# A hybrid decoder block on one core: scores of two heads in turn on two halves of TensorE's rows, PSUM pools of 3, 4 and 1 banks, a weight load moved up

## The chip, the core and the metric

The kernel runs on one core of one Trainium2 chip. The metric is the device time of one execution in microseconds; shown times are medians of a few runs. Engines are named as the profile names them: PE (matmul; PEld is its weight load), DVE, ACT, POOL, and SP, which here only issues DMAs. PSUM has eight banks, into which PE writes; a bank holds 512 fp32 numbers in each of its 128 partitions.

## What is computed

One decoder block over 16 meta tokens and 512 tokens of width 2048, all in fp32. One input projection feeds a state-space mixer (S5) and attention of 16 heads of 64; both results are normalised, concatenated, projected back, and a gated MLP with a short causal convolution follows. The part that the change touches most is attention, which is stick-breaking instead of softmax:

```python
def _stick_breaking_block(q_blk, qpos, k, v, kpos):
    scale = 1.0 / math.sqrt(ATTN_HEAD_DIM)
    z = jnp.einsum('bqhd,bkhd->bhqk', q_blk, k).astype(jnp.float32) * scale
    valid = (kpos[None, :] < qpos[:, None])[None, None]
    log_keep = jnp.where(valid, jax.nn.log_sigmoid(-z), 0.0)
    suffix = lax.cumsum(log_keep, axis=3, reverse=True) - log_keep
    w = jnp.where(valid, jnp.exp(jax.nn.log_sigmoid(z) + suffix), 0.0)
    return jnp.einsum('bhqk,bkhd->bqhd', w.astype(v.dtype), v)
...
        proj = hn @ w_in[i]
        u = proj[..., :SSM_WIDTH]
        q, k, v = jnp.split(proj[..., SSM_WIDTH:], 3, axis=-1)
...
        mixed = jnp.concatenate([rmsnorm(y_ssm, g_ssm_out[i]), rmsnorm(y_attn, g_attn_out[i])], axis=-1)
        h = h + mixed @ w_out[i]
```

## The kernel before

All activations lie with channels on the partitions and the 528 positions along the free dimension. An fp32 product is made of three matmuls on a rounded part and a remainder of each factor: high by high, high by low, low by high (`mm3`, L320 to L322). Weights come as blocks of 128 x 1024; ACT rounds a block (L242, `wh<-wr`), DVE takes the remainder (L117, `wl<-wr,wh`). `dense` runs over the blocks of one output tile of 128 channels, its positions as two halves of 256 to 264, so that a block is used for 48 matmuls.

The order of everything is written out by hand; no scheduler moves an instruction, and each engine works its own queue in order. What isn't dense work (the S5 mixer, then attention) is a generator, a *lane*. After nearly each trio of dense matmuls `pulse` adds 1.4 ns per column to a credit, and for each `period` of credit it takes one step of the lane. `PERATT` is that period in attention. While `hold` is set, during the last Q projection and the GLU of the mixer, the lane stands still.

Attention goes by four units of four heads (two pairs p, in a pair the heads i = 0, 1, whose 64 channels lie on partitions 0 to 63 and 64 to 127). `prep` splits K and Q into high and low parts and transposes V. A unit's items are: chunk 0 of the queries with all heads, chunk 1 with heads 0 and 1, then 2 and 3, chunks 2 and 3 with each head alone, and None for the last 16 queries. With chunk j go 128(j+1) keys. An item passes through
- `stage_a`: PE puts a mask into a bank of the pool psz (L961) and adds the scores (L977; L969 for chunk 0, in plain fp32), ACT makes the logarithm of the sigmoid (L105);
- `stage_a2`: DVE adds (L999), scans (L1002) and subtracts (L117, `at<-z,at`), which is the last read of the z bank;
- `stage_b`: PE transposes into another z bank (L1029; L1019 for None), ACT takes the exponential;
- `stage_c`: PE multiplies by V into a bank of psy (L1068), and DVE copies the sum out (L1075; L1072 for None).

A unit starts an item every second step of the lane, and in that step stand, in this order: a of item n, c of n-3, b of n-2, a2 of n-1. For a head i the Q operand of L977 is a tile of 128 rows in which the other head's 64 rows are zero; POOL writes the zeros (L902, L903), ACT and DVE the two halves (L907, L117). In chunk 0 each product goes to the 64 rows of its head alone, as a tile of half the array.

PSUM: three banks psd ("d") for dense sums, three psz ("z") for the lanes, two psy ("y") for the products with V, for some dense sums (`dbank`: two of five, while two lanes are left) and for sums of squares (`rms_steps`, L366). A new tile takes a bank that is free by the written order, or the next one to become free, and its first writer waits for the last reader of the tile that was there.

At the start SP issues the x tiles (L1152) and the first three weight blocks in turn, then the rest of x, the constants, and the fourth block from `ahead` (L198). The sum of squares of x ends in L366.

Of the kernel before, what the change touches and what calls it, by code (L numbers as in the profile page):

```python
# [34 lines left out]
PERATT = 950.0  # L35
# [25 lines left out]
def build(tc, io, nslots=67, manual=True):  # L61
    nc = tc.nc
    ctx = ExitStack()
    with ctx:
# [6 lines left out]
        psz = ctx.enter_context(tc.tile_pool(name="psz", bufs=3, space=PSUM))  # L71
        psy = ctx.enter_context(tc.tile_pool(name="psy", bufs=2, space=PSUM))
# [43 lines left out]
        def sub(e, out, a, b):  # L116
            e.tensor_tensor(out, a, b, op=ALU.subtract)  # L117
# [210 lines left out]
        turn = [2]  # L328
# [30 lines left out]
        def rms_steps(out, acc, parts, width, pool=(psy, "y"), last=()):  # L359
# [4 lines left out]
            for i, (a, b) in enumerate(parts):  # L364
                ps = bank([P, b - a], *pool)
                PE.matmul(ps, ones, acc[:, a:b], start=True, stop=not last)  # L366
# [497 lines left out]
        class Unit:  # L864
# [19 lines left out]
            def prep(self):  # L884
# [5 lines left out]
                for p in range(2):  # L890
                    dct = {}
                    for nm, base, n in (("A", 13, 244), ("B", 257, 256), ("T", 512, 16)):

                        if nm == "T":
                            hl = [small([P, 4, 16], "qt", F32R, bufs=8) for x in range(2)]
                            for x in hl:
                                G.memset(x.bitcast(U32), 0)
                            h0 = 2 * p
                        else:
                            hl = [slot([P, 2, n], F32R) for _ in range(2)]  # L900
                            for x in hl:
                                G.memset(x[0:64, 1, :].bitcast(U32), 0)  # L902
                                G.memset(x[64:128, 0, :].bitcast(U32), 0)  # L903
                            h0 = 0
                        for i in range(2):
                            r = slice(64 * i, 64 * i + 64)
                            S.copy(hl[0][r, h0 + i, :], qf[p][r, base : base + n])  # L907
                            sub(V, hl[1][r, h0 + i, :], qf[p][r, base : base + n], hl[0][r, h0 + i, :].bitcast(F32))
                        dct[nm] = (hl[0], hl[1], base)
                    self.qs.append(dct)  # L910
                    yield
# [16 lines left out]
            chunks = [("A", 13, 116), ("A", 129, 128), ("B", 257, 128), ("B", 385, 128)]  # L928
            items = [(0, (0, 1, 2, 3)), (1, (0, 1)), (1, (2, 3))] + [(j, (x,)) for j in (2, 3) for x in range(4)] + [None]

            def stage_a(self, it):

                if it is None:
                    n, m = 64, L
                    z = slot([P, L])[:64]
                    for x in range(2):
                        b = bank([64, 264], psz, "z")
                        for p in range(2):
                            (kh, kl), (qh, ql, _) = self.ks[p], self.qs[p]["T"]
# [11 lines left out]
                else:  # L951
                    j, hs = it
                    name, a, n = self.chunks[j]
                    k = P * (j + 1)
                    m = len(hs) * k

                    nb, lead = (2, mask0) if j == 0 else (1, mask)
                    nh = len(hs) // nb
                    zs = [bank([P, nh, k], psz, "z")[:n] for _ in range(nb)]
                    for b in zs:  # L960
                        PE.matmul(  # L961
                            b[:, :, k - P :], identb[:, :n], lead.unsqueeze(1).to_broadcast([P, nh, P]),
                            start=True, stop=False, skip_group_check=True,
                        )
                    for x, hd in enumerate(hs):
                        p, i = hd // 2, hd % 2
                        if j == 0:
                            r = slice(64 * i, 64 * i + 64)
                            PE.matmul(  # L969
                                zs[i][:, p, :], self.qf[p][r, a : a + n], self.kf[p][r, :k],  # L970
                                start=False, stop=p == 1, skip_group_check=True,
                            )
                            continue
                        (kh, kl), (qh, ql, base) = self.ks[p], self.qs[p][name]
                        r = slice(a - base, a - base + n)
                        for i_, (qq, kk) in enumerate(((qh, kh), (qh, kl), (ql, kh))):
                            PE.matmul(  # L977
                                zs[0][:, x, :], qq[:, i, r], kk[:, :k],
                                start=False, stop=x == nh - 1 and i_ == 2, skip_group_check=True,
                            )  # L980
# [30 lines left out]
            def stage_b(self, it):  # L1011
# [13 lines left out]
                n = self.chunks[j][2]  # L1025
# [8 lines left out]
            def stage_c(self, it):  # L1034
# [17 lines left out]
                _, a, n = self.chunks[j]  # L1052
# [127 lines left out]
        for k in range(5, KT):  # L1180
            load_x(k)
# [3 lines left out]
        split_x(1)  # L1185

# [516 lines left out]
```

## Time and profile before

| | us |
|---|---|
| median of 3 runs | 2210.28 |
| their range | 2209.03 to 2213.31 |
| the profiled execution, whole | 2212.19 |
| its span | 2210.4 |
| PE busy | 2167.5 |
| DVE busy | 1576.3 |
| ACT busy | 1040.3 |

The mixer fills the time up to some 377 us beside the input projection, attention runs from there to about 690 us beside the rest of the input projection, the GLU and the first half of the output projection, and the MLP takes the rest. The clock granted to TensorE was 0.994 in the mean. Rows of the timeline give start, length, engine, line and operation with `out<-in`, then sizes and count; brackets hold the engine's idle time just before, and what ended it. Matmuls overlap in the array, so the distance between two starts is what one costs in a row of them, and not its length.

### The profile page before, as it was taken

Reading aid. Unit: us, or ns where it says so; the run is one execution under the profiler, and the core shown is the slowest. Engines: PE = TensorE matmul, PEld = TensorE weight load, DVE = VectorE, ACT = ScalarE, POOL = GpSimd, SP = SyncE. Lnnn points to the kernel's source line nnn. Section 1 sums busy time; section 2 is a strip of 40 time slices with the busy share of each in tenths; the row PEclk is TensorE's granted clock in tenths of the full one; section 3 lists DMA queues with packets and bytes.
Section 4 is the critical chain, followed back from the end, with each engine's and each line's share of the span. In section 5 each row is a group of like instructions: output and inputs, shape, how many; then the busy total and the mean of one; then the engine's idle time right before and its main releaser. Section 6 shows DMA issues by size and latency. Waiting matters only on the chain.

```text
span 2210.4 us, 39830 instructions
## 1 busy us (share of the span) xinstructions
PE 2167.5 (98%) x16196; PEld 2055.5 (93%) x16196; DVE 1576.3 (71%) x2395; ACT 1040.3 (47%) x1664; POOL 227.6 (10%) x354
## 2 busy tenths in 40 slices
PE   8999999999999999999999999999999999999997
PEld 8999999899888989999999999999999888888887
DVE  7977885776786778877887787788778544444464
ACT  6154445666564555555545545555555222222235
POOL 0000000102122221111111111111110000000004
PEclk9999999999999999999999999999999999999999
DMA  5433234242332357777777777777677533333342
GB/s 207 124 111 116 98 102 140 97 156 77 106 111 96 124 169 190 205 184 194 199 194 196 193 202 187 193 195 200 193 197 207 170 127 117 117 116 120 115 143 77
DMA packets 118807, 335.11 MB, mean 152 GB/s; under 512 B 13024, under 2 KB 25696, under 8 KB 118624
## 3 DMA queue, kind: packets, MB, share of 16 engines
q1 hardware_dynamic: 100288, 269.56, 37.2%
q0 software_dynamic: 17472, 61.89, 13.6%
q8 instruction: 127, 2.08, 0.4%
q10 hardware_dynamic: 864, 1.11, 0.2%
q14 instruction: 56, 0.46, 0.1%
HBM read 300.23 MB, written 32.28 MB: 150 GB/s over the span
## 4 chain that ended last, share of the span: by engine, by line
PE 63%; DVE 2%; issue 1%; ACT 1%; POOL 0%; DVEq 0%; ACTq 0%; POOLq 0%
PE d L321 15%; PE d L320 15%; PE d L322 15%; PE z L321 4%; PE z L320 4%; PE z L322 4%; PE y L321 2%; PE y L320 2%; PE y L322 2%; DVE s L117 0%; DVE wl L117 0%; DVE s L114 0%; ACT wh L242 0%; DVE s L111 0%; ACT s L1359 0%
## 5 line engine op out<-in xcount | busy, mean ns | idle before, releaser
L320 PE MATMUL d<-s,wh 128*128 128x258 f32 (+4 forms) x3360 | 1035.9, 308 | 10.0 <-ACT wh L242 5.7
L321 PE MATMUL d<-s,wh 128*128 128x258 f32 (+4 forms) x3360 | 1028.0, 306 | 2.3 <-DVE s L403 1.7
L322 PE MATMUL d<-s,wl 128*128 128x258 f32 (+4 forms) x3360 | 1026.4, 305 | 1.2 <-DVE wl L117 1.2
L320 PEld LDWEIGHTS d<-s,wh 128*128 128x128 f32 x3360 | 637.1, 190 | 40.5 <-ACT wh L242 5.7
L321 PEld LDWEIGHTS d<-s,wh 128*128 128x128 f32 x3360 | 640.4, 191 | 31.8 <-DVE s L403 2.3
L322 PEld LDWEIGHTS d<-s,wl 128*128 128x128 f32 x3360 | 640.1, 191 | 30.0 <-DVE wl L117 1.9
L242 ACT CAST wh<-wr 128x1024 fp32r<-128x1024 f32 (+2 forms) x209 | 197.6, 946 | 428.1 <-PE d L321 337.4
L117 DVE TENSOR_TENSOR wl<-wr,wh 128x1024 fp32r<-128x1024 f32 (+2 forms) x209 | 231.5, 1108 | 88.1 <-ACT wh L242 87.8
L114 DVE TENSOR_TENSOR s<-s,d 128x512 f32<-128x512 f32 (+2 forms) x176 | 103.6, 590 | 263.3 <-PE d L322 253.0
L320 PE MATMUL z<-s,wh 128*128 128x258 f32 (+1 forms) x752 | 214.7, 286 | 0.5 <-ACT s L1434 0.5
L321 PE MATMUL z<-s,wh 128*128 128x258 f32 (+1 forms) x752 | 214.1, 285 | 0.0
L322 PE MATMUL z<-s,wl 128*128 128x258 f32 (+1 forms) x752 | 213.0, 283 | 0.5 <-DVE wl L117 0.5
L322 PE MATMUL y<-s,wl 128*128 128x258 f32 (+1 forms) x656 | 185.5, 283 | 1.2 <-DVE wl L117 1.2
L320 PE MATMUL y<-s,wh 128*128 128x258 f32 (+1 forms) x656 | 186.5, 284 | 0.0
L321 PE MATMUL y<-s,wh 128*128 128x258 f32 (+1 forms) x656 | 186.1, 284 | 0.0
L117 DVE TENSOR_TENSOR wl<-wu,wh 128x1024 fp32r<-128x1024 f32 x132 | 161.4, 1223 | 3.3 <-ACT wh L242 2.7
L114 POOL TENSOR_TENSOR s<-s,s 128x514 f32<-128x514 f32 (+1 forms) x73 | 83.4, 1143 | 697.5 <-ACT s L105 582.7
L242 ACT CAST wh<-wu 128x1024 fp32r<-128x1024 f32 x132 | 138.8, 1052 | 32.5 <-ACT s L105 32.4
L322 PEld LDWEIGHTS z<-s,wl 128*128 128x128 f32 x752 | 144.0, 191 | 0.7 <-DVE wl L117 0.7
L321 PEld LDWEIGHTS z<-s,wh 128*128 128x128 f32 x752 | 143.9, 191 | 0.0
L320 PEld LDWEIGHTS z<-s,wh 128*128 128x128 f32 x752 | 142.7, 190 | 0.7 <-ACT s L1434 0.7
L117 DVE TENSOR_TENSOR wl<-wu_s,wh 128x1024 fp32r<-128x1024 f32 x88 | 107.9, 1226 | 41.3 <-ACT wh L242 41.3
(224 smaller groups left out, 2896.1 us busy)
## 6 DMA issues: line engine op xcount, KB each, us to landing
wu<-w_up SPq DMA_DIRECT2D x132, 512.0 KB, 5.2
wu_s<-w_up SPq DMA_DIRECT2D x88, 512.0 KB, 4.7
wu_s<-w_up POOLq DMA_DIRECT2D x88, 512.0 KB, 7.0
wr<-w_down SPq DMA_DIRECT2D x96, 384.0 KB, 2.9
wr<-w_in SPq DMA_DIRECT2D x63, 512.0 KB, 4.1
wr<-w_out SPq DMA_DIRECT2D x32, 512.0 KB, 3.7
fact<-s POOLq DMA_DIRECT2D x44, 256.0 KB, 2.7
s<-fact SPq DMA_DIRECT2D x44, 256.0 KB, 3.4
```

What stands on the lines that cost most here:

```text
L114: e.tensor_tensor(out, a, b, op=ALU.add)
L117: e.tensor_tensor(out, a, b, op=ALU.subtract)
L242: S.copy(hi[:, r], raw[:, r])
L320: PE.matmul(ps, whi, xhi, start=start, stop=False, **kw)
L321: PE.matmul(ps, whi, xlo, start=False, stop=False, **kw)
L322: PE.matmul(ps, wlo, xhi, start=False, stop=stop, **kw)
```

## The change

Seven edits come together.

1. `PERATT` goes from 950 to 900.
2. psz has four banks instead of three, psy one instead of two.
3. `dbank` takes the y bank once in four calls, and a z bank in its second call; `rms_steps` takes a z bank for its second half.
4. `prep` splits Q of a pair whole, 128 x 500, with one ACT and one DVE instruction. Only the last 16 queries keep the zeroed tiles.
5. `stage_a` makes the scores of heads 0 and 1 of a pair together, each on its own 64 rows, the two heads in turn for each of the three products, into two z banks. In chunks 2 and 3 the item of the even head does this for both, and the item of the odd head takes over the second bank (`self.second`). Each bank gets its own mask.
6. The fourth weight block is fetched behind x tile 10 and the constants, ahead of x tiles 11 to 15.
7. Line numbers move: the masks are L958 (before L961), all scores L969, the transposes L1026 (L1029), the products with V L1065 (L1068), DVE's part L996, L999, L117 (L999, L1002, L117), x loads L1149 (L1152).

```diff
-PERATT = 950.0
+PERATT = 900.0
...
-        psz = ctx.enter_context(tc.tile_pool(name="psz", bufs=3, space=PSUM))
-        psy = ctx.enter_context(tc.tile_pool(name="psy", bufs=2, space=PSUM))
+        psz = ctx.enter_context(tc.tile_pool(name="psz", bufs=4, space=PSUM))
+        psy = ctx.enter_context(tc.tile_pool(name="psy", bufs=1, space=PSUM))
...
-            return bank(shape, psy, "y") if len(lanes) == 2 and turn[0] % 5 > 2 else bank(shape)
+            if len(lanes) != 2 or (turn[0] > 2 and turn[0] % 4 != 2):
+                return bank(shape)
+            return bank(shape, psz, "z") if turn[0] == 2 else bank(shape, psy, "y")
...
-                    for nm, base, n in (("A", 13, 244), ("B", 257, 256), ("T", 512, 16)):
...
-                            hl = [slot([P, 2, n], F32R) for _ in range(2)]
-                            for x in hl:
-                                G.memset(x[0:64, 1, :].bitcast(U32), 0)
-                                G.memset(x[64:128, 0, :].bitcast(U32), 0)
...
+                    hi, lo = slot([P, 500], F32R), slot([P, 500], F32R)
+                    S.copy(hi, qf[p][:, 13:513])
+                    sub(V, lo, qf[p][:, 13:513], hi.bitcast(F32))
+                    dct["Q"] = (hi, lo)
...
+                    if hs[0] % 2 == 0:
+
+                        lead, nh = (mask0, 2) if j == 0 else (mask, 1)
+                        zs = [bank([P, nh, k], psz, "z")[:n] for _ in range(2)]
...
+                                for i in range(2):
+                                    r = slice(64 * i, 64 * i + 64)
+                                    PE.matmul(
+                                        zs[i][:, p if j == 0 else 0, :], qq[r, o : o + n], kk[r, :k],
+                                        start=False, stop=p == 1 if j == 0 else i_ == 2, skip_group_check=True,
+                                    )
+                        if j > 1:
+
+                            self.second = zs.pop()
+                    else:
+                        zs = [self.second]
...
-        for k in range(5, KT):
+        for k in range(5, 11):
             load_x(k)
         nc.sync.dma_start(consts, io["consts"])
         split_x(0)
         split_w(0)
         split_x(1)
+        fetch(3)
+        for k in range(11, KT):
+            load_x(k)
```

Three places show how instructions stand. First, SP's queue at the start of the program: `s_..<-xT` are the x tiles, `wr_..<-w_in` the weight blocks. Before, from the ninth x tile on:

```order
L1152 DMA s_119<-xT 128x528
L1152 DMA s_121<-xT 128x528
L1152 DMA s_123<-xT 128x528
L1152 DMA s_125<-xT 128x528
L1152 DMA s_127<-xT 128x528
L1152 DMA s_129<-xT 128x528
L1152 DMA s_131<-xT 128x528
L1182 DMA consts<-consts 128x256
L198 DMA wr_208<-w_in 128x1024
L198 DMA wr_210<-w_in 128x1024
```

And in the changed kernel, from the same tile:

```order
L1149 DMA s_119<-xT 128x528
L1149 DMA s_121<-xT 128x528
L1179 DMA consts<-consts 128x256
L198 DMA wr_138<-w_in 128x1024
L1149 DMA s_140<-xT 128x528
L1149 DMA s_142<-xT 128x528
L1149 DMA s_144<-xT 128x528
L1149 DMA s_146<-xT 128x528
L1149 DMA s_148<-xT 128x528
L198 DMA wr_210<-w_in 128x1024
```

The fourth block (wr_208, now wr_138) and the constants have passed the last five x tiles; the fifth block keeps its place.

Second, PE in the first unit, from the masks of the third item (chunk 1, heads 2 and 3) to the transposes of the first. The dense matmuls around are left out; a bracket names the engines whose semaphores the instruction waits for. Before:

```order
L961 LDWEIGHTS identb [waits DVE_49]
L961 MATMUL z_5002<-mask,identb 128x2x128 [waits PE_49]
L977 MATMUL z_5002<-s_4794,s_4849 128x256 [waits Pool_49]
L977 MATMUL z_5002<-s_4795,s_4849 128x256
L977 MATMUL z_5002<-s_4794,s_4850 128x256 [waits Pool_49]
L977 MATMUL z_5002<-s_4794,s_4849 128x256
L977 MATMUL z_5002<-s_4795,s_4849 128x256
L977 MATMUL z_5002<-s_4794,s_4850 128x256
L1029 MATMUL z_5014<-consts,at_4978 128x116 [waits DVE_49,PE_49]
L1029 MATMUL z_5014<-consts,at_4978 128x116 x3
```

And changed:

```order
L958 LDWEIGHTS identb [waits DVE_49]
L958 MATMUL z_4970<-mask,identb 128x128 [waits PE_49]
L958 LDWEIGHTS identb [waits DVE_49]
L958 MATMUL z_4971<-mask,identb 128x128 [waits PE_49]
L969 MATMUL z_4970<-s_4794,s_4833 128x256
L969 MATMUL z_4971<-s_4794,s_4833 128x256
L969 MATMUL z_4970<-s_4795,s_4833 128x256
L969 MATMUL z_4971<-s_4795,s_4833 128x256
L969 MATMUL z_4970<-s_4794,s_4834 128x256
L969 MATMUL z_4971<-s_4794,s_4834 128x256
L1026 MATMUL z_4985<-consts,at_4946 128x116 [waits DVE_49,PE_49]
L1026 MATMUL z_4985<-consts,at_4946 128x116 x3
```

The item now takes two banks and waits for DVE at each. The transposes wait for DVE in both; before, their bank's last reader is DVE's subtraction of the first item, whose result they read anyway, and now it is DVE's first subtraction of the second item (`at_4992<-z_4931`).

Third, PE some 20 dense matmuls on: the scores of the fourth item, the products with V of the first (`y`), and the transposes of the second. Before:

```order
L961 LDWEIGHTS identb [waits DVE_49]
L961 MATMUL z_5054<-mask,identb 128x128 [waits PE_49]
L977 MATMUL z_5054<-s_4790,s_4825 128x384
L977 MATMUL z_5054<-s_4791,s_4825 128x384
L977 MATMUL z_5054<-s_4790,s_4826 128x384
L1068 MATMUL y_5063<-s_5019,s_4886 64x116 [waits Activation_49]
L1068 MATMUL y_5063<-s_5019,s_4886 64x116
L1068 MATMUL y_5063<-s_5019,s_4915 64x116 x2
L1029 MATMUL z_5070<-consts,at_5021 128x128 [waits PE_49]
L1029 MATMUL z_5070<-consts,at_5021 128x128 x3
```

And changed:

```order
L969 MATMUL z_5024<-s_4790,s_4804 128x384
L969 MATMUL z_5025<-s_4790,s_4804 128x384
L969 MATMUL z_5024<-s_4791,s_4804 128x384
L969 MATMUL z_5025<-s_4791,s_4804 128x384
L969 MATMUL z_5024<-s_4790,s_4805 128x384
L969 MATMUL z_5025<-s_4790,s_4805 128x384
L1065 MATMUL y_5038<-s_4990,s_4851 64x116 x2
L1065 MATMUL y_5038<-s_4990,s_4880 64x116 x2
L1026 MATMUL z_5045<-consts,at_4992 128x128 [waits DVE_49]
L1026 MATMUL z_5045<-consts,at_4992 128x128 x3
```

The transposes now wait for DVE. The instruction that frees their bank is the first subtraction of the third item (`at_5052<-z_4970`), and in DVE's queue it stands behind the copies of y_5038, two additions and two scans. These two places are the same in all four units.

Over the whole attention the lane's steps come sooner among the dense calls: the last of them stands two dense calls earlier than before, each of 48 matmuls, and in the second unit the None item's `stage_a` and `stage_a2` stand ahead of the hold, where before they stood behind it.

More of the change, by code (lines that the diff above doesn't have):

```diff
@@ L364, in rms_steps @@
             for i, (a, b) in enumerate(parts):
-                ps = bank([P, b - a], *pool)
+                ps = bank([P, b - a], *(pool if i == 0 or pool[0] is psd else (psz, "z")))
                 PE.matmul(ps, ones, acc[:, a:b], start=True, stop=not last)
@@ L891, in prep @@
                     dct = {}
[L892 to L909 removed]
+                    hi, lo = slot([P, 500], F32R), slot([P, 500], F32R)
+                    S.copy(hi, qf[p][:, 13:513])
+                    sub(V, lo, qf[p][:, 13:513], hi.bitcast(F32))
+                    dct["Q"] = (hi, lo)
+                    hl = [small([P, 4, 16], "qt", F32R, bufs=8) for x in range(2)]
+                    for x in hl:
+                        G.memset(x.bitcast(U32), 0)
+                    for i in range(2):
+                        r = slice(64 * i, 64 * i + 64)
+                        S.copy(hl[0][r, 2 * p + i, :], qf[p][r, 512:528])
+                        sub(V, hl[1][r, 2 * p + i, :], qf[p][r, 512:528], hl[0][r, 2 * p + i, :].bitcast(F32))
+                    dct["T"] = hl
                     self.qs.append(dct)
@@ L952, in stage_a @@
                     j, hs = it
-                    name, a, n = self.chunks[j]
+                    a, n = self.chunks[j]
                     k = P * (j + 1)
                     m = len(hs) * k
[L957 to L968, printed above, removed]
+                    if hs[0] % 2 == 0:
+                        lead, nh = (mask0, 2) if j == 0 else (mask, 1)
+                        zs = [bank([P, nh, k], psz, "z")[:n] for _ in range(2)]
+                        for b in zs:
                             PE.matmul(
-                                zs[i][:, p, :], self.qf[p][r, a : a + n], self.kf[p][r, :k],
-                                start=False, stop=p == 1, skip_group_check=True,
-                            )
[L973 to L980, printed above, removed]
+                                b[:, :, k - P :], identb[:, :n], lead.unsqueeze(1).to_broadcast([P, nh, P]),
+                                start=True, stop=False, skip_group_check=True,
+                            )
+                        for p in (0, 1) if j == 0 else (hs[0] // 2,):
+                            (kh, kl), (qh, ql) = self.ks[p], self.qs[p]["Q"]
+                            for i_, (qq, kk, o) in enumerate(
+                                ((self.qf[p], self.kf[p], a),) if j == 0 else ((qh, kh, a - 13), (qh, kl, a - 13), (ql, kh, a - 13))
+                            ):
+                                for i in range(2):
+                                    r = slice(64 * i, 64 * i + 64)
+                                    PE.matmul(
[6 more added lines that the diff above has]
+                        zs = [self.second]
@@ L1024, in stage_b @@
                 j, hs = it
-                n = self.chunks[j][2]
+                n = self.chunks[j][1]
                 nb = len(hs) * (j + 1)
@@ L1051, in stage_c @@
                 j, hs = it
[L1052 removed]
+                a, n = self.chunks[j]
                 if hs[-1] % 2 == 0:
```

6 lines of the change are left out of this document (3 added, 3 removed).

## The prediction

> **What bounds the kernel now.** The page's first part comes first: the span and how much of it each engine works.
>
> ```profile
> span 2210.4 us, 39830 instructions
> PE 2167.5 (98%) x16196; PEld 2055.5 (93%) x16196; DVE 1576.3 (71%) x2395; ACT 1040.3 (47%) x1664; POOL 227.6 (10%) x354
> ```
>
> PE leaves 43 us of the span, so the change is worth what it takes from PE's own work, from PE's waits, and from the time in which PE is clocked down. The view of waits, for PE, has the second (total, times, longest); the view of windows the third (busy time by engine, then PEclk, DMA share, GB/s).
>
> ```profile
> PE z L961 <- DVE at L117: 5.7, 5, 3.3
> PE z L1019 <- DVE at L117: 4.3, 3, 2.2
> PE y L366 <- DVE s L114: 2.9, 1, 2.9
> PE d L321 <- DVE s L403: 1.7, 3, 0.8
> PE d L320 <- DVE s L111: 1.5, 2, 1.0
> ...
> 0.00:20.00 20.00, 14.31 (x97) 14.22 (x98) 10.56 (x14) 11.17 (x16) 2.02 (x16) 1.00 0.91 332
> 45.00:48.45 3.45, 3.45 (x16) 3.35 (x15) 3.04 (x9) 1.58 (x4) 0.91 (x2) 0.51 0.27 72
> 377.00:690.00 313.00, 300.56 (x2586) 278.94 (x2585) 231.69 (x381) 197.71 (x369) 52.36 (x87) 0.98 0.33 108
> 704.00:714.00 10.00, 7.35 (x40) 6.55 (x41) 8.01 (x11) 3.61 (x6) 3.89 (x2) 0.83 0.22 76
> ```
>
> Attention (377 to 690 us) waits for banks that DVE's last subtraction of an item (L117, at<-z) gives back. The 2.9 us wait at L366 is followed by 3.45 us at a clock of 0.51: 0.49 x 3.45 is 1.7 us, and some **1.55 us** of it is lost (in the rest PE stood anyway). The 0.98 over attention is 313 x 0.02 = 6.3 us, four such stretches; the 0.83 of 704 to 714 is one more. So a wait of 2 to 3 us costs half as much again.
>
> **The fourth weight load.** The timeline, SP's queue and then the two splitting engines and PE (start, length, and in brackets the idle time before).
>
> ```profile
> 5.96 8.39 SPq L1152 DMA_DIRECT2D s<-xT  x11
> 15.45 9.94 SPq L198 DMA_DIRECT2D wr<-w_in  x4
> 22.72 1.05 ACT L242 CAST wh<-wr 128x1024 fp32r<-128x1024 f32 x1 [6.32 <-DMA wr<-w_in]
> 23.80 1.23 DVE L117 TENSOR_TENSOR wl<-wr,wh 128x1024 fp32r<-128x1024 f32 x1 [5.55 <-ACT wh L242]
> 44.23 1.38 PE L366 MATMUL y<-s,consts 128*128 128x264 f32 x4 [2.94 <-DVE s L114]
> ```
>
> The block is issued behind eleven x tiles, and DVE stands for 5.55 us until ACT has rounded it; then DVE works until L366 has its sum. Eleven tiles go out in 8.39 us, so the five that the block now passes take 3.8, and it lands that much sooner: ACT has it at 18.9, and DVE's 5.55 us of idleness shrink to 1.7. From there DVE's chain is without a gap, so the sum is ready at 44.2 - 3.8 = 40.4, before PE is free (44.23 - 2.94 = 41.3). The five passed tiles come some 1.5 us later (a block is 512 KB, a tile 270), and DVE reaches them only behind the eleven earlier ones. The wait of 2.94 goes whole, and with it the 1.55 of half clock: **-4.5**. Late next is nothing on PE; the block after it was not waited for. Bounds: -2.9 if the clock falls anyway, +0.5 if DVE then stands for the passed tiles instead.
>
> **The scores.** The timeline of PE for one old item of the last chunk, and for a place where the old kernel already works with row halves (chunk 0).
>
> ```profile
> 406.06 0.23 PE L961 MATMUL z<-mask,identb 128*128 128x128 bf16 x1
> 406.10 0.94 PE L977 MATMUL z<-s,s 128*128 128x512 f32 x3
> 406.97 0.88 PE L1068 MATMUL y<-s,s 128*64 128x128 f32 x12
> ...
> 380.58 0.29 PE L321 MATMUL d<-s,wh 128*128 128x264 f32 x1
> 380.71 0.28 PE L322 MATMUL d<-s,wl 128*128 128x264 f32 x1
> 380.83 0.38 PE L961 MATMUL z<-mask,identb 128*116 128x256 bf16 x2
> 381.14 0.70 PE L969 MATMUL z<-s,s 64*116 64x128 f32 x8
> 381.77 0.39 PE L320 MATMUL d<-s,wh 128*128 128x264 f32 x1
> ```
>
> An old item, mask to the next stage, takes 406.97 - 406.06 = 0.91 us, 0.10 of it the change into the column halves that follow at L1068: 0.81, of which I take three times 0.23 for 512 columns (the dense rows start 0.12 apart for 264) and 0.12 for the mask. Two heads are 1.63. The eight half-row records at 381.14 run 0.70 us though the fp32 product with 128 columns is two passes: four pairs, each costing one pass; the halves **overlap**. From 380.83 to 381.77 the block takes 0.94 where its pieces make 0.65, so entering and leaving the mode costs 0.3 to 0.4. A pair of the new form is then 3 x 0.23 + masks and entry 0.30 = 0.99, a gain of 0.64; leaving falls on L1068, which pays a change already. Eight pairs of 512 columns: -5.1. For 384 columns the pieces scale to 0.83 against 1.31: eight times -0.47 is -3.8. Chunk 1 (256 columns, four pairs a unit before and after) gains three passes of 0.12 per pair and pays one more mask and both changes: +0.14 for each unit's first pair, 0 for the second, +0.6. Sum **-8.2**. Bounds: -4 if every change costs 0.4; +4 if the fp32r halves go one after the other, which no row here excludes, as 381.14 is plain fp32.
>
> The Trainium skill, TensorEngine Tiling (Array Packing), Key Properties, speaks against this part: a change of tiling mode, not just of tile, drains TensorE. Read strictly, the step from row halves to L1068's column halves is a full drain too, on top of both others, and the scores would bring -4 and not -8.2; the trace shows one direct change from whole rows only, and no row for this one.
>
> **The new waits.** With four z banks two items in chunk 1 take two each, and then the pool is full. The order of the change shows two places, in each of the four units, where PE comes to a bank whose last reader is one item nearer than before. The rows of old for the first place, PE and then DVE:
>
> ```profile
> 387.57 0.28 PE L961 MATMUL z<-mask,identb 128*128 128x256 bf16 x1 [0.69 <-DVE at L117]
> 388.41 0.56 PE L1029 MATMUL z<-consts,at 116*128 116x116 f32 x4
> ...
> 387.12 0.73 DVE L117 TENSOR_TENSOR at<-z,at 116x256 f32<-116x256 f32 x2
> 387.76 0.68 DVE L999 SCALAR_TENSOR_TENSOR at<-z,at 128x512 f32<-128x512 f32 x1
> 388.48 1.27 DVE L1002 TENSOR_TENSOR_SCAN at<-steady,at 128x256 f32<-128x256 f32 x2
> 389.78 0.69 DVE L117 TENSOR_TENSOR at<-z,at 128x512 f32<-128x512 f32 x1
> ```
>
> Old: the masks of the third item wait for chunk 0's first subtraction, and its transposes (L1029) follow at 388.41. New: both banks of chunk 0 are needed (0.3 later), and the transposes need the first bank of the second item, whose subtraction is now two of 256 columns: 389.78 + half of 0.69 + 0.1 = 390.23. That is 1.8 us later than 388.41; in the third unit, which waits 3.3 already, I count 0.9, in the others 1.9: **+6.5**. The second place, behind the matmuls of L1068 for chunk 0:
>
> ```profile
> 392.12 0.62 PE L1068 MATMUL y<-s,s 128*64 128x116 f32 x8
> 392.67 0.66 PE L1029 MATMUL z<-consts,at 128*128 128x128 f32 x4
> ...
> 393.44 0.45 DVE L1075 COPY s<-y 128x115 f32<-128x115 f32 x2
> 393.81 0.68 DVE L999 SCALAR_TENSOR_TENSOR at<-z,at 128x512 f32<-128x512 f32 x1
> 394.52 1.27 DVE L1002 TENSOR_TENSOR_SCAN at<-steady,at 128x256 f32<-128x256 f32 x2
> 395.83 0.69 DVE L117 TENSOR_TENSOR at<-z,at 128x512 f32<-128x512 f32 x1
> ```
>
> Old: the transposes at 392.67 take a bank that ACT has emptied long before. New: they need the first bank of the third item. DVE copies the y bank out first, which waits for L1068 itself, and then does that item: from 393.44 to half of the subtraction at 395.83 are 2.75 us, and 0.15 for the two hand-overs: 2.9 us in which PE can do nothing, since the transposes stand at the head of its queue and all dense work is behind them. Four units: **+11.6**. Bounds for both together: 6 (DVE runs ahead because PE is late) and 24. Elsewhere the bank's last reader is an item away, as before; that DVE's items of 512 columns (0.68 + 1.26 + 0.69) now come in faster turn gets +2, by the new 900 against 950.
>
> Each unit thus has two stops of 2.5 to 3 us. By the row at 45.00 such a stop halves the clock for 3.4 us if it fills over half of a stretch; I give six of eight, 9.3 us, against the 6.3 now: **+3.0**.
>
> **Where the lane's end falls.** By the 900 the attention's steps come 5% sooner. Two places gain. First, the GLU's hold, PE before it resumes:
>
> ```profile
> 546.56 1.09 PE L1068 MATMUL y<-s,s 128*64 128x128 f32 x14 [0.72 <-ACT s L105]
> 549.86 0.56 PE L1019 MATMUL z<-consts,at 64*128 64x64 f32 x5 [2.21 <-DVE at L117]
> ```
>
> Here the last item of the second unit runs with no dense work between its stages. In the new order its scores and DVE's part stand ahead of the hold: -2.9 here, and -1.2 at the other waits of that kind (4.3 in all at L1019): **-4.1**. Second, the lane's last splits (L403, L111 in the waits above) come two dense calls of 5.8 us earlier, and are no longer waited for: 1.7 + 1.5, a clock stretch of 1.55, and 0.5 of small ones: **-5.3** (bounds -3.2 and -5.7).
>
> **Hidden.** The Q split loses POOL's zeroing, and ACT and DVE halve their instructions; none of these ended a PE wait in the rows above. 0, or -1 where DVE starts an item sooner. The single y bank: its next writer is an item behind the copy that frees it, 0 to +1.
>
> **Sum.** -4.5 - 8.2 + 6.5 + 11.6 + 2 + 3.0 - 4.1 - 5.3 = +1.0 on the profiled execution's 2212.2 us (its span and 1.8 around it), which stands 1.9 above the median of 2210.28. On the median: **2211 us**, no change that a measurement can tell (about 0.2%, 4.4 us).
>
> **Rivals.** *The new waits are cheap*: DVE comes to both places ahead, the second costs 1 us and not 2.9, half of the new clock loss goes, and so do the +2: -7.6 - 4 - 2 from the sum, 2198. For it: DVE is 74% busy in attention (231.69 of 313), and the Q split takes six short instructions a unit from it. Against: the copies ahead of it wait for PE's own matmuls, which a faster DVE doesn't bring sooner. 0.25.
>
> *The stops fall astride*: a stop of 2.9 us that lies half in one 3.45 us stretch and half in the next leaves both busy enough, and no clock is lost at the new places: 2211 - 9.3 = 2202. For it: attention has four low stretches now for eight waits at L961 and L1019. Against: 44.23, where 2.94 were enough. 0.05. The Trainium skill, TensorE: Matmul & The Clock Gate, Part 1, has the clock fall after a whole idle window of some 3.4 us, which would give this case; the row at 45.00 stands against it.
>
> *Stops feed on each other*, the slower side: each of the eight halves the clock (+3.1), PE's slower dense work makes the next item late at ACT and DVE, and the first place costs 3 us in every unit (12 for 6.5, +5.5), the second 3.4 (+2): 2221. It decides if PE's waits in attention pass 32 us. For it: the third unit's first place waits 3.3 already. Against: a PE at half clock gives DVE time. 0.18.
>
> *Row halves in turn*: fp32r passes do not overlap and the scores cost +4 where I have -8.2: 2223; it decides if a pair of 512 columns takes over 1.63 us. Against: 381.14. 0.11.
>
> *The load is not sooner*: the DMA engines share their bandwidth among all that is queued, and it lands as late as before: 2215.5. For it: 332 GB/s are moved in the first 20 us, at a DMA share of 0.91. 0.07.
>
> My own case has 0.34. The range goes from the cheap waits to the stops, leaving out the outer part of either: 2199 to 2222. Faster by over 0.2%: the cheap waits, falling astride, 0.02 of mine: 0.32. Slower: the stops, row halves in turn, half of the load and 0.02 of mine: 0.34. Within: 0.34.
>
> **What would show it.** DVE's idle before the fourth block below 2 us, and PE's wait at the first sum gone. A row-half pair of 512 columns near 0.99 us from mask to the next stage. PE waits at the transposes for L117 near 2.9 us, four times, and near 2.6 in two pieces at the first place, four times; a clock of 0.97 over attention; no wait for L403 near the end of attention. If the transposes wait under 1.5 us, or the pair takes over 1.3, this sum is wrong.

## The result, and the profile after

The changed kernel takes 2229.39 us (median of 4 runs, 2228.11 to 2230.80), the kernel before beside it 2209.88. The ratio is 1.0085, with a 95% interval of 1.0068 to 1.0103: slower, outside the range of 2199 to 2222. The profiled execution took 2228.46 us. The page's first part:

```profile
span 2226.7 us, 39757 instructions
PE 2163.8 (97%) x16204; PEld 2049.5 (92%) x16204; DVE 1567.0 (70%) x2387; ACT 1032.5 (46%) x1648; POOL 209.6 (9%) x290
```

And the first rows of PE's waits (total, times, longest):

```profile
PE z L1026 <- DVE at L117: 25.5, 14, 4.2
PE d L320 <- ACT wh L242: 5.6, 1, 5.6
PE z L958 <- DVE at L117: 4.7, 6, 1.6
PE d L320 <- DVE s L111: 2.8, 2, 2.0
PE z L1016 <- DVE at L117: 2.4, 2, 1.8
```

Every engine is busy for less time than before, and the span is 16.3 us longer. PE waits 25.5 us at the transposes (L1026), where the view of before has no row for the transposes (L1029).

The dense matmuls come in the same order in both kernels, so the start of the n-th of them is a common clock. The time between two of them can be split: the idle time of PE; half of the non-idle time in which the clock stood at half; the distance from start to start that is left, by kind. For three stretches of the profiled executions, before and after, in us:

| dense matmuls | 0 to 300 | 300 to 2450 (mixer) | 2450 to 4300 (attention, and the last splits) | 4300 to 14680 |
|---|---|---|---|---|
| whole | 44.7, 39.9 | 319.4, 318.2 | 348.6, 372.0 | 1477.1, 1476.1 |
| PE idle | 2.9, 0.0 | 0.2, 0.0 | 15.6, 38.8 | 6.2, 6.3 |
| low clock | 1.7, 0.0 | 0.0, 0.0 | 7.9, 15.4 | 0.0, 0.0 |
| masks and scores | | | 35.6, 27.5 | |

The start gains 4.8 us and the score matmuls 8.1. Attention loses 23.1 us to waits and 7.5 to the clock; the view of windows has its clock at 0.95 between the first transpose of V and some ten us behind the last item, where the kernel before had 0.98:

```profile
371.09:704.00 332.91, 296.92 (x2544) 271.34 (x2543) 222.65 (x372) 189.60 (x353) 37.10 (x34) 0.95 0.31 99
566.00:584.00 18.00, 11.09 (x61) 9.78 (x61) 8.31 (x21) 5.71 (x13) 0.00 (x0) 0.72 0.39 134
```

The second row is the worst place, the start of the third unit. The timeline of PE there, without the dense rows, and of DVE:

```profile
565.50 0.56 PE L958 MATMUL z<-mask,identb 128*128 128x128 bf16 x2 [0.72 <-DVE at L117]
565.99 0.62 PE L969 MATMUL z<-s,s 64*128 64x256 f32 x6
570.81 1.01 PE L1026 MATMUL z<-consts,at 116*128 116x116 f32 x4 [4.19 <-DVE at L117]
...
576.46 0.80 PE L1065 MATMUL y<-s,s 128*64 128x116 f32 x8
579.98 0.87 PE L1026 MATMUL z<-consts,at 128*128 128x128 f32 x4 [2.72 <-DVE at L117]
...
565.05 0.72 DVE L117 TENSOR_TENSOR at<-z,at 116x256 f32<-116x256 f32 x2
565.70 1.21 DVE L117 TENSOR_TENSOR wl<-wr,wh 128x1024 fp32r<-128x1024 f32 x1
566.83 0.41 DVE L372 TENSOR_SCALAR s<-d 128x258 f32<-128x258 f32 x1
567.17 0.41 DVE L379 SCALAR_TENSOR_TENSOR s<-s 128x258 f32<-128x258 f32 x1
567.61 0.43 DVE L111 TENSOR_TENSOR s<-s,s 128x258 f32<-128x258 f32 x1
568.07 0.43 DVE L384 SCALAR_TENSOR_TENSOR rstd<-s,s 128x258 f32<-128x258 f32 x1
568.42 0.75 DVE L996 SCALAR_TENSOR_TENSOR at<-z,at 128x256 f32<-128x256 f32 x2
569.08 1.26 DVE L999 TENSOR_TENSOR_SCAN at<-steady,at 128x256 f32<-128x256 f32 x2
570.26 0.73 DVE L117 TENSOR_TENSOR at<-z,at 128x256 f32<-128x256 f32 x2
577.31 0.46 DVE L1072 COPY s<-y 128x115 f32<-128x115 f32 x2 [6.32 <-PE y L1065]
577.69 0.74 DVE L996 SCALAR_TENSOR_TENSOR at<-z,at 128x256 f32<-128x256 f32 x2
578.35 1.26 DVE L999 TENSOR_TENSOR_SCAN at<-steady,at 128x256 f32<-128x256 f32 x2
579.53 0.73 DVE L117 TENSOR_TENSOR at<-z,at 128x256 f32<-128x256 f32 x2
```

The first place is the transposes at 570.81: they start when the first of the two subtractions at 570.26 is done, and that item stands behind a weight split and half of a normalisation (565.70 to 568.42). In the old kernel such work stood ahead of chunk 0's item, and PE waited 3.32 us for that one at the masks. The second place is 579.98. DVE was idle for 6.32 us until PE's products (L1065) were there to be copied, and only then came to the item on which PE's next instruction waits: each engine waited for the other in turn. The second place waits exactly 2.72 us in each of the four units.

### The profile page after: what moved, and what is told of

Its sections match the earlier page's. It is cut to its first block, busy times and chain, and to the rows that moved or that the text cites. A ratio compares the mean times of both kernels' runs of the same rounds, so it can differ in the third digit from the quotient of the medians.

```text
span 2226.7 us, 39757 instructions
## 1 busy us (share of the span) xinstructions
PE 2163.8 (97%) x16204; PEld 2049.5 (92%) x16204; DVE 1567.0 (70%) x2387; ACT 1032.5 (46%) x1648; POOL 209.6 (9%) x290
## 3 DMA queue, kind: packets, MB, share of 16 engines
q10 hardware_dynamic: 864, 1.11, 0.2%
## 4 chain that ended last, share of the span: by engine, by line
PE 62%; DVE 2%; ACT 1%; issue 1%; DVEq 0%; ACTq 0%
PE d L321 15%; PE d L320 15%; PE d L322 15%; PE z L321 4%; PE z L320 4%; PE z L322 4%; PE y L321 2%; PE y L322 2%; PE y L320 2%; DVE s L117 0%; DVE wl L117 0%; ACT s L1359 0%; ACT wh L242 0%; ACT s L105 0%; DVE s L114 0%
## 5 line engine op out<-in xcount | busy, mean ns | idle before, releaser
L320 PE MATMUL d<-s,wh 128*128 128x258 f32 (+4 forms) x3456 | 1063.5, 308 | 12.1 <-ACT wh L242 5.6
L321 PE MATMUL d<-s,wh 128*128 128x258 f32 (+4 forms) x3456 | 1057.4, 306 | 1.2 <-DVE s L117 1.2
L322 PE MATMUL d<-s,wl 128*128 128x258 f32 (+4 forms) x3456 | 1052.7, 305 | 1.2 <-DVE wl L117 1.2
L320 PEld LDWEIGHTS d<-s,wh 128*128 128x128 f32 x3456 | 656.4, 190 | 43.8 <-ACT wh L242 7.8
L322 PEld LDWEIGHTS d<-s,wl 128*128 128x128 f32 x3456 | 660.2, 191 | 29.9 <-DVE wl L117 1.8
L321 PEld LDWEIGHTS d<-s,wh 128*128 128x128 f32 x3456 | 658.2, 190 | 30.9 <-DVE s L117 2.5
L117 DVE TENSOR_TENSOR wl<-wr,wh 128x1024 fp32r<-128x1024 f32 (+2 forms) x209 | 232.8, 1114 | 86.5 <-ACT wh L242 86.5
L321 PE MATMUL z<-s,wh 128*128 128x258 f32 (+1 forms) x768 | 219.5, 286 | 0.0
L320 PE MATMUL z<-s,wh 128*128 128x258 f32 (+1 forms) x768 | 218.7, 285 | 0.5 <-ACT s L1434 0.5
L322 PE MATMUL z<-s,wl 128*128 128x258 f32 (+1 forms) x768 | 217.7, 283 | 0.5 <-DVE wl L117 0.5
L117 DVE TENSOR_TENSOR wl<-wu,wh 128x1024 fp32r<-128x1024 f32 x132 | 161.4, 1223 | 2.8 <-ACT wh L242 2.7
L320 PE MATMUL y<-s,wh 128*128 128x258 f32 (+1 forms) x544 | 155.7, 286 | 0.0
L322 PE MATMUL y<-s,wl 128*128 128x258 f32 (+1 forms) x544 | 154.4, 284 | 1.2 <-DVE wl L117 1.2
L321 PE MATMUL y<-s,wh 128*128 128x258 f32 (+1 forms) x544 | 154.5, 284 | 0.0
L321 PEld LDWEIGHTS z<-s,wh 128*128 128x128 f32 x768 | 146.9, 191 | 0.0
L320 PEld LDWEIGHTS z<-s,wh 128*128 128x128 f32 x768 | 145.1, 189 | 0.7 <-ACT s L1434 0.7
L117 DVE TENSOR_TENSOR wl<-wu_s,wh 128x1024 fp32r<-128x1024 f32 x88 | 107.5, 1222 | 41.8 <-ACT wh L242 41.8
```

What stands on the lines that cost most here:

```text
L320: PE.matmul(ps, whi, xhi, start=start, stop=False, **kw)
L321: PE.matmul(ps, whi, xlo, start=False, stop=False, **kw)
L322: PE.matmul(ps, wlo, xhi, start=False, stop=stop, **kw)
```

## The experiments

Theory: the loss is the bank waits at the two places of chunk 1 and the low clock behind them, and the scores and the load are gains. Rivals: the shorter period overruns DVE; the single y bank or the dense banks taken away cost the time; the row halves are worth nothing. Each run below was compared with the kernel before on the same chip, whose median lay between 2210.6 and 2211.0. The runs come from several chips; where two changed kernels are compared, the difference is that of their medians, and the ratios to the kernel before give the same within 1 us.

### One part alone, on the kernel before

The load (`e1_fetch`): the diff's last part alone.

```diff
-        for k in range(5, KT):
+        for k in range(5, 11):
             load_x(k)
...
+        fetch(3)
+        for k in range(11, KT):
+            load_x(k)
```

> The kernel before with the fourth weight load moved up and nothing else. If the load does in the changed kernel what it seems to (there the place of the first 300 dense matmuls is 4.8 us earlier), this one is 4.8 us faster than before, at about 2205. If the load needs something else of the change, it stays at 2210.

Measured: 2208.10 us, ratio 0.9986 (0.9977 to 0.9996), a gain of 3 us by the ratio (2.5 by the medians) where 4.8 were expected; 4.8 is just inside the interval. In its trace PE's 2.94 us at the first sum of squares and the stretch of low clock are gone: the first 300 dense matmuls take 40.5 us for 44.7, though the mixer behind them takes 321.0 for 319.4. The load needs nothing else of the change.

The banks (`e2_banks`): pools of 3, 4 and 1, with `dbank` and `rms_steps` of the change, old scores.

> The kernel before with the PSUM pools at 3, 4 and 1, and dbank and the second half of the sum of squares as in the change; scores, Q split, period and load as before. My theory: the lost time comes from score items that take two z banks each, so with one bank per item the fourth bank is slack and the time is that of before or 1 to 2 us less (2208 to 2211; the mixer's z banks gave 1 us in the changed kernel). Rival: the single y bank, or the dense banks taken away, cost the time; then it is well over 2212.

Measured: 2210.52, ratio 1.0000 (0.9990 to 1.0009). The single y bank and the smaller share of dense sums in it cost nothing on balance: in the trace 1.3 us are gained in the mixer, and attention takes 348.7 us for 348.6, though the two longest waits have other names (L1031 for L117, 6.3 us in all, and the products with V for the copies, 3.3). So the banks and the new turns alone do not make the loss; it needs the items that take two banks as well.

### The period

`e3_950`: the changed kernel with `PERATT` at 950.

> The changed kernel with the lane's period back at 950. My theory: the two waits of chunk 1 lie inside one step of the lane each, so a longer period leaves them (2.7 us at the second place, four times) and takes only some of the other waits: 2224 to 2229. Rival: DVE is overrun by the faster turn, and the waits fall away with 950: below 2218.

Measured: 2234.33, ratio 1.0104 (1.0089 to 1.0119); by the medians 5 us slower than the changed kernel, which neither side had expected. The two intervals overlap, so the time alone does not show 900 to be the better period here; in the traces attention with the last splits takes 375.4 us for 372.0. The second place waits 2.72 us four times as before, so a longer period does not help it; the first place gets worse in the second unit (0.42 and 2.81 us) and the third (3.35 and 5.39), the None item falls behind the hold again (0.73 and 2.30), and the last splits are waited for again. The rival that DVE is overrun by 900, and that 950 takes the loss away, is out.

### A fifth z bank

`e4_z5`: the changed kernel with pools of 2, 5 and 1.

```diff
-        psd = ctx.enter_context(tc.tile_pool(name="psd", bufs=3, space=PSUM))
-        psz = ctx.enter_context(tc.tile_pool(name="psz", bufs=4, space=PSUM))
+        psd = ctx.enter_context(tc.tile_pool(name="psd", bufs=2, space=PSUM))
+        psz = ctx.enter_context(tc.tile_pool(name="psz", bufs=5, space=PSUM))
```

> The changed kernel with pools of 2, 5 and 1 instead of 3, 4 and 1 (a sum of squares and a third of the last projection's sums use z banks in place of d). With a fifth z bank the transposes find a bank that ACT has emptied in both places of chunk 1. My theory: 10.9 us at the second place, 8.5 at the first and most of the new 7.5 us of low clock go: 2200 to 2205, faster than before. Rivals: the scores' own matmuls or the period make the loss, then it stays above 2220; two banks for dense sums make new waits at L320, then it lies between.

Measured: 2211.63, ratio 1.0004 (0.9994 to 1.0013): 18 us faster than the changed kernel, and not below the old one as expected. PE's waits show both the half that held and the half that didn't:

```profile
PE d L320 <- DVE s L111: 10.7, 8, 3.2
...
PE z L1032 <- DVE at L117: 5.1, 8, 1.9
PE z L964 <- DVE at L117: 4.9, 6, 1.5
PE d L320 <- DVE s L114: 4.1, 3, 1.9
```

The transposes (now L1032) wait 5.1 us in all for 25.5, and attention with the last splits takes 341.1 us for 372.0. But with two dense banks PE waits for DVE to empty them: the mixer takes 329.0 us for 318.2. The last rival named in the expectation was right beside the theory.

`e5_z5b`: the same, with dense sums where banks are free. In the mixer's phase they go to d, y, z, d in turn, and from the end of attention's items on every third to z.

```diff
-            if len(lanes) != 2 or (turn[0] > 2 and turn[0] % 4 != 2):
-                return bank(shape)
-            return bank(shape, psz, "z") if turn[0] == 2 else bank(shape, psy, "y")
+            if len(lanes) == 2:
+                return [bank, lambda s: bank(s, psy, "y"), lambda s: bank(s, psz, "z"), bank][turn[0] % 4](shape)
+            return bank(shape, psz, "z") if free_z[0] and turn[0] % 3 == 0 else bank(shape)
```

> The kernel of e4_z5 (pools 2, 5 and 1), but the dense sums of the mixer's phase take d, y, z, d in turn, and from the end of attention's items on every third dense sum takes a z bank. In e4_z5 PE waited some 6.8 us plus 3.4 us of low clock in the mixer's phase, and 3.9 us near the end of attention, for dense banks (L320 behind DVE's L111), with the rest of the scores' gain in place. If that is what holds it at 2211.6, this one is at 2196 to 2201. If the waits for two dense banks only move elsewhere, it stays above 2206.

Measured: 2193.14, ratio 0.9920 (0.9905 to 0.9934), 3 us better than the expected range. The mixer is at 318.6 us again, and attention with the last splits at 337.5, of which 16.6 are waits and 3.4 low clock. This is faster than both kernels.

### The order in DVE's queue

`e6_a2first`: the changed kernel; in each step of the lane a2 is issued ahead of b and c.

```diff
-                    for f, it in todo.pop(now[0], []):
+                    for f, it in sorted(todo.pop(now[0], []), key=lambda x: x[0].__name__ != "stage_a2"):
```

> The changed kernel, with one change of order: in a step of the lane DVE's part of an item (a2) is issued ahead of the products with V and their copies (c) and of the transposes (b). My theory of the second place: the transposes wait 2.72 us because DVE's work for the third item stands behind the copies, which wait for PE; DVE stands idle for 6.3 us just before them. With a2 ahead the four waits of 2.72 fall under 0.5 and some low clock goes: 2229 - 10.9 - 3 = 2215 (2211 to 2219); the first place keeps its 13.8 us. Rival: DVE has no time for that item before the copies, then the transposes still wait over 1.5 us and the time stays above 2222.

Measured: 2212.67, ratio 1.0009 (0.9999 to 1.0018), 17 us faster than the changed kernel by one line that moves copies behind an item. The size is as expected, but the waits at the second place did not all fall under 0.5: they are 1.74, 1.40, under 0.15 and 0.83, 4.0 for 10.9. In the first unit:

```profile
387.46 0.43 DVE L111 TENSOR_TENSOR s<-d,rstd 128x264 f32<-128x264 f32 x1
387.81 0.75 DVE L996 SCALAR_TENSOR_TENSOR at<-z,at 128x256 f32<-128x256 f32 x2
388.47 1.26 DVE L999 TENSOR_TENSOR_SCAN at<-steady,at 128x256 f32<-128x256 f32 x2
389.65 0.73 DVE L117 TENSOR_TENSOR at<-z,at 128x256 f32<-128x256 f32 x2
390.29 0.45 DVE L1072 COPY s<-y 128x115 f32<-128x115 f32 x2
...
390.10 0.66 PE L1026 MATMUL z<-consts,at 128*128 128x128 f32 x4 [1.74 <-DVE at L117]
```

The copies are behind the item now, but ahead of it a weight split and an eviction still stand. Some 5 us of the gain are clock, 10.2 us for 15.4. So the copies' place in the queue is shown as the cause of most of the second wait; what is left of it is DVE's other work.

`e7_both`: e5_z5b with this order.

> e5_z5b with the order of e6_a2first. With five z banks the second place is free already, so the order should change little: within 3 us of e5_z5b. If copies and DVE's part of an item also collide elsewhere in a unit, it is 3 us or more faster; if PE's products wait for the single y bank because the copies come later, slower.

Measured: 2192.04, ratio 0.9915 (0.9900 to 0.9930), 1.1 us better than e5_z5b and not told apart from it. Two effects of the order nearly cancel in its trace: the transposes wait 2.8 us for 5.2, and the products with V now wait 2.2 us for the copies of the single y bank.

### What the row halves and the period are worth when banks do not bind

`e8_oldscores`: e5_z5b with the old scores and Q split.

> e5_z5b with the scores and the Q split of the kernel before (whole rows, zeroed halves, one bank an item); banks, dense turns, load and period as in e5_z5b. In the changed kernel masks and scores take 27.5 us of PE against 35.6, 8.1 less. If that is a gain wherever banks do not bind, this one is 6 to 10 us slower than e5_z5b, 2199 to 2203. If the banks alone made e5_z5b fast and the row halves are worth nothing, it is within 3 us of 2193.

Measured: 2203.94, ratio 0.9968 (0.9956 to 0.9980), 10.8 us slower than e5_z5b, a little beyond the dearer end of what was expected. The stage's non-dense matmuls take 93.1 us of starts for 84.1, and the low clock 5.8 for 3.4. So the row halves are worth some 9 us of PE's time, and the banks, the places of the dense sums, the load and the period together the other 7 of the 18 gained on the kernel before; no run takes these apart.

`e9_950` and `e10_850`: e7_both with other periods.

> e7_both with the period at 950. In the changed kernel 950 put the None item of the second unit behind the hold and the lane's last splits back in PE's way (stage of attention 3.4 us longer). If the period is worth that by itself, this one is 3 to 6 us slower than e7_both, 2195 to 2198; if it only steered how the bank waits fell, it is within 2 us of 2192.

> e7_both with the period at 850. If the ends of the lane are what the period is good for, and they are out of PE's way at 900 already, it is within 2 us of e7_both; if the faster turn makes DVE late for the items of chunks 2 and 3, it is 2 to 6 us slower, 2194 to 2198.

Measured: 2200.99 (0.9938 to 0.9968 of before) and 2202.64 (0.9953 to 0.9981), 9.0 and 10.6 us slower than at 900: both misses, beyond even the dearer side. With 950 the timeline of PE shows the old picture again, in the order hold, third unit, last splits:

```profile
538.11 1.09 PE L1072 MATMUL y<-s,s 128*64 128x128 f32 x14 [0.76 <-ACT s L105]
541.40 0.51 PE L1023 MATMUL z<-consts,at 64*128 64x64 f32 x5 [2.21 <-DVE at L117]
560.14 0.62 PE L965 MATMUL z<-mask,identb 128*128 128x128 bf16 x2 [3.32 <-DVE at L117]
...
693.83 0.39 PE L321 MATMUL d<-s,wh 128*128 128x258 f32 x1 [0.76 <-DVE s L412]
695.10 0.39 PE L321 MATMUL d<-s,wh 128*128 128x258 f32 x1 [0.65 <-DVE s L412]
```

In the stage of attention with 950, PE's waits sum to the same 16.3 us as at 900, and what is lost is clock: 8.1 us for 3.4, since three of them are long (3.32, 2.21 and 1.88), where the longest at 900 is 1.71. The stage makes 4.8 us of the 8.2 between the two profiled executions; another 3.9 lie behind it, spread over the MLP, where 400 dense matmuls take some 0.1 us more of 48. Nothing in the traces ties this part to the period.

With 850 one wait for DVE's subtraction, at masks near the start of the third unit, is 5.75 us long, and attention takes 345.4 us for 335.9, with 8.7 us more of waits. The period is worth what it makes of the hold, the third unit and the lane's end. Of the three, 900 is the best, by 4.8 us of attention against 950 and by 9.5 against 850: no trend, but a place where these meet well.

## Why the prediction was wrong

Its sum was +1.0 us on the profiled execution, and +16.3 came. Term by term, from the waits in the two timelines:

| term | predicted | measured | how measured |
|---|---|---|---|
| the load | -4.5 | -4.8 | first 300 dense matmuls |
| scores | -8.2 | -8.1 | masks and scores, 35.6 to 27.5 |
| first place | +6.5 | +8.5 | 13.8 now, 5.3 of such waits before |
| second place | +11.6 | +10.9 | 4 x 2.72 |
| DVE late in chunks 2 and 3 | +2 | +4.1 | 5.5 now, 1.4 before (0.7 of it at the None items' scores) |
| None items | -4.1 | -1.9 | 3.2 now, 5.0 before |
| last splits | -5.3 | -1.9 | waits 2.8 for 3.2, one low stretch less |
| clock in attention | +3.0 | +9 | ten low stretches of 3.4 us for four |
| GLU's splits, mixer, rest | 0 | +0.4 | +1.5, -1.3, -1.0, dense starts +1.2 |

**What was right.** The load does what was said, and alone as well (e1_fetch). So do the row halves: a pair of 512 columns takes 1.11 us from its masks to the products with V, where 0.99 and 0.10 for the change at L1065 were forecast:

```profile
597.78 0.28 PE L958 MATMUL z<-mask,identb 128*128 128x128 bf16 x2
598.00 0.96 PE L969 MATMUL z<-s,s 64*128 64x512 f32 x6
598.89 0.88 PE L1065 MATMUL y<-s,s 128*64 128x128 f32 x12
```

Six matmuls of 512 columns start within 0.89 us (598.00 to 598.89), where an old item's three on whole rows took 0.87 (406.10 to 406.97): fp32r halves overlap. The strict reading of the Trainium skill, TensorEngine Tiling (Array Packing), Key Properties, by which the step from row halves to column halves is one more full drain, is not borne out in size: only 0.12 us (1.11 less 0.99) are left for it here. Both new waits are there, in all four units, with the instruction named as their releaser, and the second with its size (2.72 for 2.9). The rivals of cheap waits, halves in turn and an idle load are out. So is the rival of stops astride as a whole, but the first unit shows its mechanism, as said below.

**The step that failed** is the clock term, the number of low stretches that follow the stops. No term alone makes the miss of 15.3 us, but this one has the largest part, 6.0; the lane's end has 3.4, and the None items, DVE's lateness in chunks 2 and 3 and the first place some 2 each. The prediction gave six of eight stops one low stretch each, 9.3 us. The six came: both stops of the first unit lost no clock, and all of the other three units did. But the stretches were ten, 15.4 us. The first places of the third and the fourth unit took two each, and two waits elsewhere took one each: 1.85 us at transposes of chunk 2, and 1.80 at the third unit's None item, which had waited 1.85 and lost a stretch in the kernel before too. The old third unit's wait of 3.32 us was already followed by a low stretch of double length (567.26 to 574.08), two of the four stretches that the prediction counted over attention, so the trace of the kernel before had a stop with more than one. The other three executions of the changed kernel had mean granted clocks of 0.989 and 0.990 for the profiled 0.991, so ten is not a stray count.

Rows of the view of windows show what decides (busy times of PE, PEld, DVE, ACT and POOL; then PEclk, DMA share and GB/s):

```profile
385.73:389.14 3.41, 2.16 (x23) 1.53 (x21) 2.77 (x7) 1.63 (x4) 0.00 (x0) 1.00 0.00 0
389.14:392.56 3.42, 1.95 (x17) 1.95 (x17) 1.74 (x4) 1.23 (x3) 0.00 (x0) 1.00 0.00 0
440.34:443.75 3.41, 1.84 (x16) 1.47 (x17) 2.68 (x7) 2.21 (x5) 0.00 (x0) 1.00 0.09 35
443.76:447.17 3.41, 3.41 (x18) 3.15 (x16) 1.22 (x1) 1.19 (x2) 0.00 (x0) 0.50 0.00 0
566.63:570.04 3.41, 0.00 (x0) 0.00 (x0) 3.34 (x9) 1.92 (x4) 0.00 (x0) 1.00 0.55 146
570.05:576.87 6.82, 6.06 (x31) 5.37 (x33) 0.94 (x3) 0.86 (x2) 0.00 (x0) 0.50 0.75 278
```

In the first unit the wait of 2.72 us lies astride two stretches (1.25 and 1.47 us idle), and neither is followed by a low one. In the second unit a wait of 1.46 us lies whole in one, with 0.10 at the masks before it, and the next is at half clock; in the first unit the same wait has 1.39 in one stretch, and the clock stays. That the first unit lost nothing was luck of place, and so was the count of six.

The time came near the rival of stops that feed on each other, which had 0.18, and its sign came too: PE's waits in attention pass 32 us (38.8 less 2.8 for the last splits are 36.0). Its mechanism, that PE at half clock makes the next item late, is not what the runs show. The 1.80 us stood in the kernel before. In e7_both PE waits at the two late transposes of the third unit before its first low stretch at 599.52 (1.54 us at 570.91 and 0.87 at 585.66, for 1.85 and 0.95 here). In e3_950 the fourth unit's first place waits 2.94 us, as here, with no low stretch in the 50 us before it. That the stops cause the clock's loss, and not the other way about, e4_z5 shows: without them it is 3.4 us.

**The first place** was mis-sized in the third and fourth units, 4.9 and 4.5 us for the 4.2 and 2.8 that the prediction's terms make: the price of the wait was taken from the first unit, where DVE's queue is clear between two items. In the third a weight split and half of a normalisation stand there, and in the fourth a weight split and an eviction:

```profile
643.23 1.01 PE L1026 MATMUL z<-consts,at 116*128 116x116 f32 x4 [2.93 <-DVE at L117]
...
639.38 1.21 DVE L117 TENSOR_TENSOR wl<-wr,wh 128x1024 fp32r<-128x1024 f32 x1
640.51 0.41 DVE L111 TENSOR_TENSOR s<-d,rstd 128x258 f32<-128x258 f32 x1
```

In the fourth unit they stood between the same items in the kernel before (633.34 to 634.81), so its own timeline had the price.

**DVE's lateness in chunks 2 and 3** had +2 without a sum behind it, and was 4.1; its largest wait (1.85 us, at 593.74) is there with five z banks as well (1.94 in e5_z5b).

**The lane's end** was a wrong reading. The splits did come earlier, and no wait for them is left, as forecast. But the prediction asked only what the old wait needed, and not what is late next: DVE's chain of splits (0.69 and 0.74 us a tile) now holds up the evictions of dense sums instead. These rows are of PE, then of DVE:

```profile
720.67 0.36 PE L320 MATMUL d<-s,wh 128*128 128x258 f32 x1 [2.01 <-DVE s L111]
...
718.51 0.74 DVE L405 SCALAR_TENSOR_TENSOR s<-s,vec,s 128x514 fp32r<-128x514 f32 x1
719.43 0.75 DVE L405 SCALAR_TENSOR_TENSOR s<-s,vec,s 128x514 fp32r<-128x514 f32 x1 [0.18 <-issue]
720.11 0.42 DVE L111 TENSOR_TENSOR s<-d,rstd 128x256 f32<-128x256 f32 x1
```

The same chain ends the wait, through a bank and not through data. e5_z5b, which gives dense sums z banks there, has 1.4 us in all of waits for L111 where this kernel has 2.8.

**The None items.** The one at the hold went, as forecast. The prediction counted a further 1.2 us at the other waits of its kind; the third unit's stayed (1.80 for 1.85), since no reason was given why it should go, and there was none. The first unit's grew (0.60 for 0.25), and a transpose of V (L917) now waits 0.77 us for ACT.

What is open: the longer period makes the stage of attention 3.4 us longer in the changed kernel and 4.8 in e7_both, most of it low clock (19.0 us for 15.4, and 8.1 for 3.4), but where its waits fall is seen place by place, not from a rule; and the dense matmuls' own starts lose some 1 us in the mixer wherever the load is moved (262.8 for 261.8 us), which no run explains.

## What to carry to other kernels

When an item's demand on a ring of buffers doubles, follow the written order until the ring is full, and price each wait by all that stands in the releasing engine's queue at that place, unit by unit, not by the cleanest of them. An instruction that waits for the other engine (here a copy out of PSUM) is best issued behind work that is ready, when that work frees what the other engine needs next: one line was worth 17 us where banks were short, and with a fifth bank nothing that could be told apart. A gain on the bounding engine (8 us here) is kept only if the buffers that it costs are found elsewhere: with a fifth bank, and dense sums placed where banks are free, the same change is 18 us faster than before instead of 19 slower. A wait costs more than its length if it is long in one piece: with the same 16.3 us of waits in e7_both and e9_950, the longer period lost 4.7 us more to the clock.

## What the runs showed of the hardware

The clock falls long before PE is idle for a whole stretch of 3.4 us. The low stretches, but for the one at the program's end, are 3.413 us long or a whole multiple of it, and in each of the twelve traces their starts lie whole multiples of 3.413 us apart (in the changed kernel 443.76, two lengths later 450.58, and 35 lengths after that 570.05). So they lie on a grid that does not follow the waits. In the changed kernel, of the stretches at full clock, all seven in which PE stood for 1.8 us or more were followed by a low one, and of the eight with 1.2 to 1.6 us only one was (1.56 us, from 440.34). A wait's place on the grid thus decides as well as its length: 2.72 us halved the clock in three units and not in the first. The border is not sharp in the other traces (1.82 us without a low stretch behind it in e3_950, 0.78 with one in e6_a2first), and no run moved one wait along the grid. In the stage of attention each low stretch cost 1.5 us, and ten of them 15.4. The Trainium skill, TensorE: Matmul & The Clock Gate, Part 1, names a whole idle window of some 3.4 us as the condition; by these waits a part of one is enough.

With the same instructions the granted clock differs from one execution to the next: the kernel before had 0.993 to 0.996 in thirteen executions on one chip. An estimate from these figures is some four low stretches between the extremes, as 0.003 of 2210 us is 6.6 us, and half of a stretch is 1.7.

The 128 matmuls of the mixer at L779 (L781 after) take 13.8 us of starts with four z banks, for 15.9 with three, with no wait of PE over 0.05 us shown at them in either kernel; e2_banks has 13.8 too, and e1_fetch, with three, 15.9. No run parts the fourth bank from the new turns of the dense sums that come with it.
